# Feed-forward gate and up projections by Strassen's seven products, with the inner activations kept in float32

## The chip, the cores and the metric

The kernel runs on one core of a Trainium2 chip. The metric is the device time of one execution in microseconds (us); less is better. The time before is 1957.03 us, the median of three runs (1954.57 to 1961.09).

Five engines work beside each other and synchronise by semaphores: TensorE (PE: matmuls, and PEld: the loads of their stationary operand), VectorE (DVE), ScalarE (ACT), GpSimd (POOL) and SyncE (SP), which issues the DMAs. Each takes its own instructions strictly in the order in which the program lists them.

## The reference, cut to what matters

Two transformer-like blocks on 512 tokens of width 1024, all in float32. The part that changes is the feed-forward layer, which occurs twice (ffn1 after the first block, ffn2 at the very end):

```python
D_MODEL, SEQ, D_FF = 1024, 512, 2816

def swiglu(h, w_gu, w_down):          # w_gu: 1024 x 5632, w_down: 2816 x 1024
    gu = h @ w_gu
    g, u = jnp.split(gu, 2, axis=-1)
    return (jax.nn.silu(g) * u) @ w_down

f = swiglu(rmsnorm(h, ffn1_pre_g[l]), ffn1_w_gu[l], ffn1_w_down[l])
h = h + 0.5 * rmsnorm(f, ffn1_post_g[l])
```

## The kernel before

Every float32 product is made of three matmuls on a pair of tiles. `split` (line 79) writes a rounded copy `hi` (ScalarE, line 82) and the rest `lo = x - hi` (VectorE, line 83). A product is then hi·hi + hi·lo + lo·hi, summed in PSUM. So a weight tile arrives by DMA in a buffer `raw` (three buffers of 128x1024), is split into `whi` and `wlo`, and feeds TensorE.

In a feed-forward layer (`ffn`, line 728) the normalised input lies as the pair `a_hi`, `a_lo`, transposed, four blocks of 128 tokens by eight blocks of 128 channels. The hidden width is worked off in 11 steps of 256 columns; a step makes 256 columns of the gate g and 256 of u.

- The first step is `lead_T` (line 170): its matmuls (line 187) have 256 columns of tokens, so that it can start on tokens 0 to 255 while the norm of tokens 256 to 511 is still being made. That norm, per block of 128 tokens, is a chain VectorE, POOL, VectorE, ScalarE, VectorE, POOL, VectorE: POOL does one small instruction in it twice (`rp_r`, line 76, a power on 128x1).
- The other ten steps are two calls of `proj_T` each (line 143; matmuls at line 164): two weight tiles of 128x1024, and 2 column halves x 8 channel blocks x 3 = 48 matmuls of 512 columns. The result in PSUM is evacuated by silu on ScalarE (line 741) for g, by a multiplication on VectorE (line 748) for u, and the product is split into `hid_hi`, `hid_lo` at once.
- The down projection is `proj_X` (line 194; matmuls at line 209) through `post_pre` (line 257), in two halves of 512 output columns; the stationary operand is `hid_hi`/`hid_lo`, the moving one the weights.

A scheduler of the Tile framework sets, when the kernel is built, the order in which each engine's instructions stand. It moves instructions of different loop steps past each other, and the tile pools decide which buffer a tile takes over, hence which earlier reader a write must wait for.

Of the kernel before, what the change touches and what calls it, by code (L numbers as in the profile page):

```python
# [7 lines left out]
F32 = mybir.dt.float32  # L8
# [23 lines left out]
def block_kernel(ctx, tc, A, out, upto=99):  # L32
# [134 lines left out]
            for j in range(nj):  # L167
                consume(cc // 128 + j, banks[j][:min(128, w - j * 128), :nt * 128])

    def lead_T(groups, get, slots, splits=((0, 2), (2, 4))):  # L170

        hls = []
        for src, c0, _ in groups:
            hls.append([wload(src, kc, 4, c0, 256, slots.pop(0)) for kc in (0, 4)])
        banks = [[bank() for _ in range(2)] for _ in groups]
        for si, (t0, t1) in enumerate(splits):
            if si:
                flush()
            for g, (_, _, consume) in enumerate(groups):
                for kc in range(2):  # L180
                    hi, lo = hls[g][kc]
                    for j in range(2):
                        for k in range(4):
                            xh, xl = get(kc * 4 + k, t0, t1)
                            wh, wl = hi[:, k, j * 128:j * 128 + 128], lo[:, k, j * 128:j * 128 + 128]
                            for n, (a, b) in enumerate(((wh, xh), (wh, xl), (wl, xh))):
                                PE.matmul(banks[g][j][:, t0 * 128:t1 * 128], a, b, start=(kc + k + n + si == 0),  # L187
                                          stop=(kc == 1 and k == 3 and n == 2), skip_group_check=True)
                                tick((t1 - t0) * 128)
                if t1 == NT:  # L190
                    for j in range(2):
                        consume(j, banks[g][j])

    def proj_X(src, c0, w, get, consume, K=8, nt=NT, tail=1, kp=2, korder=None, between=None, slots=(), ready=None):

# [58 lines left out]
        else:  # L254
            later(delay, lambda: transpose_split(h, 8, pair, t))

    def post_pre(src, K, get, g_post, half_scale, g_pre, fg, last=False, dst=None, korder=None, slots=(), tail=1, delay=DELAY):

        gpost = gain(g_post)
        gpre = None if last else gain(g_pre)  # L260
        x_sb = xb["x"]
        sss = [None] * NT
        pair = None if last else (dst() if dst else new_act())
        mul, eps = (4.0 / D, 4.0 * EPS) if half_scale else (1.0 / D, EPS)

        def evac(hf):
            def f(t, bank):
                fgt = fg[:, t if hf == 0 else NT + t % 2]
                ss = sm.tile([128, 2], F32, name=f"pss{t}", bufs=1) if hf == 0 else sss[t]
                sss[t] = ss  # L270
                ACT.activation(fgt, bank, AF.Square, accum_out=ss[:, hf:hf + 1])
                V.tensor_tensor(fgt, bank, gpost[:, hf * 512:(hf + 1) * 512], op=ALU.mult)  # L272
                if hf == 1:
                    s2 = sm.tile([128, 1], F32, name="s2")
                    V.tensor_tensor(s2, ss[:, 0:1], ss[:, 1:2], op=ALU.add)
                    r = rpow(s2, mul, eps)
                    for q in range(2):
                        xs = x_sb[:, t, q * 512:(q + 1) * 512]
                        V.scalar_tensor_tensor(xs, fg[:, t if q == 0 else NT + t % 2], r, xs, op0=ALU.mult, op1=ALU.add)  # L279
                        if last:  # L280
                            nc.sync.dma_start(out[0].rearrange("(t p) d -> p t d", p=128)[:, t, q * 512:(q + 1) * 512], xs)
                    if not last:
                        prenorm_tile(x_sb[:, t], gpre, pair, t, None, delay)
            return f
        for hf in range(2):
            proj_X(src, hf * 512, 512, get, evac(hf), K=K, korder=korder, tail=max(tail, len(slots)) if hf else 1, slots=slots if hf else ())
        if delay is None:
            flush()
        return pair
# [11 lines left out]
    def first_block():  # L301
# [413 lines left out]
        def of_mb(i):  # L715
            def f():
                if not wmb:
                    wmb[0] = n2.tile([128, 4, 1024], F32R, name="wmb", tag="mb")
                return wmb[0][:, 2 * i], wmb[0][:, 2 * i + 1]
            return f  # L720
        pr = post_pre(A["w_out"], 8, act_get(mg), "norm_post", False, "ffn1_pre_g_2", fg, slots=(two("att0", "att1"), of_mb(0), of_mb(1)))
        st.close()
        return pr
# [4 lines left out]
    def ffn(pair, n, nxt, last=False):  # L728
        st = ExitStack()
        l1 = pool(f"f{n}a", 1, stack=st)  # L730
        l2 = pool(f"f{n}b", 2, stack=st)
        get = act_get(pair)
        w_gu, w_dn = A[f"ffn{n}_w_gu_2"][0], A[f"ffn{n}_w_down_2"][0]
        KF = DFF // 128
        hid = [[l1.tile([128, 2, 512], F32R, name=f"hid_{x}{f}") for x in ("hi", "lo")] for f in range(KF // 2)]
        sg = {}

        def ev_g(f0):
            def f(j, bank):
                s = l2.tile([128, 512], F32, name="sg")  # L740
                ACT.activation(s, bank, AF.Silu)
                sg[f0 + j] = s
            return f

        def ev_u(f0):
            def f(j, bank):
                s = sg.pop(f0 + j)
                V.tensor_tensor(s, s, bank, op=ALU.mult)
                split(hid[f0 // 2][0][:, j], hid[f0 // 2][1][:, j], s)
            return f  # L750
        def hget(k, t0, t1):
            return [x[:, k % 2, t0 * 128:t1 * 128].rearrange("p (t q) -> p t q", q=128) for x in hid[k // 2]]

        def slot(i):
            return lambda: [l1.tile([128, 1024], F32R, name="wsl", tag=f"hid_{x}{i}") for x in ("hi", "lo")]
        lead_T(((w_gu, 0, ev_g(0)), (w_gu, DFF, ev_u(0))), get, [None, None, slot(KF // 2 - 2), slot(KF // 2 - 1)])
# [4 lines left out]
        fg = l1.tile([128, 6, 512], F32, name="fg")  # L761
        pr = post_pre(w_dn, KF, hget, f"ffn{n}_post_g_2", True, nxt, fg, last=last, slots=[slot(i) for i in range(4)])
        st.close()
        return pr

# [3 lines left out]
    def mixer(pair, st):  # L769
# [345 lines left out]
        fg = l1.tile([128, 6, 512], F32, name="fg", tag="u2")  # L1115
        tails = [lambda: [x1.tile([128, 1024], F32R, name=f"wsl{i}") for i in range(2)]]
        g1, g2 = act_get(osT), act_get(oaT, 8)

# [28 lines left out]
    def cross(pair, l1, x1, kT, vm, st):  # L1147
# [9 lines left out]
        for hq in range(2):  # L1157
# [28 lines left out]
            for h in (hq * 2, hq * 2 + 1):  # L1186
                for e in range(2):
# [4 lines left out]
                                      start=(m + a + b == 0), stop=(m + a == 2))  # L1192
                    split(oT[0][:, :, h * 2 + e], oT[1][:, :, h * 2 + e], ob.rearrange("p (t q) -> p t q", t=NT))
        fg = l1.tile([128, 6, 512], F32, name="fg", tag="u2")
        wpt = {}

        def of(tag, i):
# [92 lines left out]
```

## Time and profile before

| | |
|---|---|
| time of three runs | 1957.03 us median, 1954.57 to 1961.09 |
| the profiled execution | 1957.59 us, span 1955.8 us |
| granted TensorE clock, mean | 0.995 |
| TensorE busy | 1903.7 us, 97% of the span |
| VectorE, ScalarE, POOL busy | 1003.9, 708.7 and 38.3 us |
| ffn1: lead step, ten steps, down projection begin at | 580.65, 598.21, 815.84 us |
| ffn2: the ten steps, down projection begin at | 1611.67, 1829.29 us |

The profile is that of one execution. Busy time says how long an engine had an instruction in flight; what limits the time is read from the chain of waits, which is followed back from the last instruction, at each step to what released it. A stretch in which the chain is one long run of matmuls is a stretch in which TensorE sets the pace.

### The profile page before, as it was taken

To read this page: it belongs to the slowest core of one execution; us is meant where nothing else is said; L and a number is where in the kernel's file an instruction comes from. 1 tells how busy PE (TensorE), PEld (TensorE's weight loads), DVE (VectorE), ACT (ScalarE), POOL (GpSimd) and SP (SyncE) were. 2 spreads that over 40 slices of the span, in tenths; PEclk is the share of its full clock that TensorE was granted. 3 is DMA by queue.
4 is the path that set the end of the run, shared out by engine and by line. 5 is a ranking of instruction groups with operands and counts; after the bars stand their busy time and mean duration, and the time that the engine had idled before them with its cause. 6 is when DMAs were issued, how large, how long until landed. Compare 5 with 4: busy or idle time off the path is not lost.

```text
span 1955.8 us, 24155 instructions
## 1 busy us (share of the span) xinstructions
PE 1903.7 (97%) x9676; PEld 1557.1 (80%) x9676; DVE 1003.9 (51%) x1712; ACT 708.7 (36%) x1190; POOL 38.3 (2%) x66
## 2 busy tenths in 40 slices
PE   7999999999999999999999999989999999999998
PEld 6778888788878888888877777667788888888887
DVE  5578833724563333323668666785464553333223
ACT  4345533223343222223545433344353432323221
POOL 0000000100000000000000000000000000000000
PEclk9999999999999999999999999999999999999999
DMA  7411033232332333333231355442262322333332
GB/s 244 130 44 34 24 106 97 88 97 87 105 100 85 97 96 97 96 96 124 83 88 44 87 134 130 125 119 76 83 192 82 99 63 87 97 97 98 97 97 86
DMA packets 153560, 191.10 MB, mean 98 GB/s; under 512 B 9732, under 2 KB 111464, under 8 KB 153320
## 3 DMA queue, kind: packets, MB, share of 16 engines
q1 hardware_dynamic: 153448, 189.56, 32.2%
q8 instruction: 76, 1.25, 0.3%
q14 instruction: 36, 0.29, 0.0%
HBM read 174.85 MB, written 2.10 MB: 90 GB/s over the span
## 4 chain that ended last, share of the span: by engine, by line
PE 81%; DVE 11%; ACT 1%; POOL 1%; issue 1%; DMA 1%; POOLq 0%; DVEq 0%; SPq 0%; ACTq 0%
PE mm L164 41%; PE mm L209 27%; PE mm L187 3%; DVE E L1067 2%; POOL rp_r L76 1%; DVE x_sb L279 1%; DVE l L1070 1%; PE ob L538 1%; DVE h L251 1%; DVE wlo L83 1%; PE s L561 1%; PE ob L924 1%; PE s L1165 1%; DVE fg L272 1%; PE mm L579 1%
## 5 line engine op out<-in xcount | busy, mean ns | idle before, releaser
L83 DVE TENSOR_TENSOR wlo<-raw,whi 128x1024 fp32r<-128x1024 f32 (+1 forms) x274 | 333.6, 1217 | 675.6 <-ACT whi L82 670.1
L82 ACT ACTIVATE whi<-raw 128x1024 fp32r<-128x1024 f32 (+1 forms) x274 | 289.0, 1055 | 692.7 <-PE mm L164 296.7
L164 PE MATMUL mm<-a_hi,wlo 128*128 128x512 f32 x1120 | 439.1, 392 | 1.9 <-DVE wlo L83 1.9
L164 PE MATMUL mm<-a_hi,whi 128*128 128x512 f32 x1120 | 440.3, 393 | 0.0
L164 PE MATMUL mm<-a_lo,whi 128*128 128x512 f32 x1120 | 439.3, 392 | 0.0
L164 PEld LDWEIGHTS mm<-a_hi,wlo 128*128 128x128 f32 x1120 | 210.8, 188 | 46.0 <-DVE wlo L83 2.4
L164 PEld LDWEIGHTS mm<-a_hi,whi 128*128 128x128 f32 x1120 | 210.7, 188 | 44.5 <-issue 2.0
L164 PEld LDWEIGHTS mm<-a_lo,whi 128*128 128x128 f32 x1120 | 210.9, 188 | 43.5 <-issue 1.7
L209 PE MATMUL mm<-whi,a_hi 128*128 128x512 f32 (+1 forms) x384 | 150.6, 393 | 2.2 <-ACT a_hi L82 2.2
L209 PE MATMUL mm<-whi,a_lo 128*128 128x512 f32 (+1 forms) x384 | 151.1, 393 | 0.0
L209 PE MATMUL mm<-wlo,a_hi 128*128 128x512 f32 (+1 forms) x384 | 149.5, 391 | 0.0
L209 PE MATMUL mm<-whi,hid_hi 128*128 128x512 f32 x288 | 112.0, 389 | 0.0
L209 PE MATMUL mm<-whi,hid_lo 128*128 128x512 f32 x288 | 112.0, 389 | 0.0
L209 PE MATMUL mm<-wlo,hid_hi 128*128 128x512 f32 x288 | 112.0, 389 | 0.0
L209 PEld LDWEIGHTS mm<-whi,a_hi 128*128 128x128 f32 x384 | 72.7, 189 | 19.0 <-ACT a_hi L82 2.8
L209 PEld LDWEIGHTS mm<-whi,a_lo 128*128 128x128 f32 x384 | 72.8, 189 | 15.2 <-issue 2.3
L209 PEld LDWEIGHTS mm<-wlo,a_hi 128*128 128x128 f32 x384 | 72.5, 189 | 14.3 <-issue 1.6
L76 POOL TENSOR_TENSOR rp_r<-rp_a,half 128x1 f32<-128x1 f32 (+1 forms) x58 | 36.8, 635 | 1891.2 <-DVE rp_a L74 1571.7
L209 PEld LDWEIGHTS mm<-whi,hid_lo 128*128 128x128 f32 x288 | 54.1, 188 | 11.3
L209 PEld LDWEIGHTS mm<-whi,hid_hi 128*128 128x128 f32 x288 | 54.1, 188 | 11.2
L209 PEld LDWEIGHTS mm<-wlo,hid_hi 128*128 128x128 f32 x288 | 54.1, 188 | 11.2
L1067 DVE TENSOR_TENSOR_SCAN E<-l,own 128x128 f32<-128x128 f32 (+2 forms) x64 | 49.6, 811 | 8.3 <-ACT l L1058 8.3
(446 smaller groups left out, 2846.6 us busy)
## 6 DMA issues: line engine op xcount, KB each, us to landing
raw<-in_w_in_dram SPq DMA_DIRECT2D x96, 512.0 KB, 3.7
raw<-in_ffn_w_gu_dram SPq DMA_DIRECT2D x88, 512.0 KB, 3.5
raw<-in_ffn_w_down_dram SPq DMA_DIRECT2D x44, 512.0 KB, 3.7
raw<-in_w_out_dram SPq DMA_DIRECT2D x24, 512.0 KB, 3.8
raw<-in_xa_wkv_dram SPq DMA_DIRECT2D x16, 512.0 KB, 4.2
raw<-in_w_ret_o_dram SPq DMA_DIRECT2D x8, 512.0 KB, 3.4
K<-kh SPq DMA_DIRECT2D x32, 128.0 KB, 2.4
K<-kl SPq DMA_DIRECT2D x32, 128.0 KB, 2.3
```

The costliest lines, as they stand in the source:

```text
L76: POOL.tensor_tensor(r[:, :n], a[:, :n], half[:, :n], op=ALU.pow)
L82: ACT.activation(hi, src, AF.Copy)
L83: V.tensor_tensor(lo, src, hi.bitcast(F32), op=ALU.subtract)
L164: PE.matmul(o, a, b, start=(kc + k == 0 and n == 0 and si == 0), stop=(kc + k == K - 1 and n == 2), skip_group_check=True)
L187: PE.matmul(banks[g][j][:, t0 * 128:t1 * 128], a, b, start=(kc + k + n + si == 0), stop=(kc == 1 and k == 3 and n == 2), skip_group_check= ...
L209: PE.matmul(banks[t][:, :w], a, b, start=(kk == 0 and n == 0), stop=(kk == K - 1 and n == 2))
L251: V.scalar_tensor_tensor(h, src, r, g, op0=ALU.mult, op1=ALU.mult)
L272: V.tensor_tensor(fgt, bank, gpost[:, hf * 512:(hf + 1) * 512], op=ALU.mult)
L279: V.scalar_tensor_tensor(xs, fg[:, t if q == 0 else NT + t % 2], r, xs, op0=ALU.mult, op1=ALU.add)
L538: m = PE.matmul(ob[64 * e:64 * e + 64, a], vv[:, j, br, g * 64:(g + 1) * 64], pT[:, e, j], start=False, stop=(br == 1 and j == nk - 1), sk ...
L561: PE.matmul(sbs[e], qS[:, h, qsl], kk[:, br, g, :W], start=(n == 0 and (e == 0 or nk > 2)), stop=(n == 1), skip_group_check=True)
L1067: V.tensor_tensor_scan(E[:, rev], l[:, off + W - 1:(off - 1) if off else None:-1], own1[:, 511:(511 - W) if W < 512 else None:-1], 1.0, op ...
```

## The change

The ten steps behind the lead step no longer call `proj_T`. Each half step (256 columns of g, or of u) is a call of `seven_T`, which takes the product of the weight tile, cut in 2 channel halves by 2 column halves (w11, w12, w21, w22), with the activations, cut in 2 token halves by 2 channel halves, as seven block products after Strassen and Winograd. A block product has 4 channel blocks x 3 = 12 matmuls of 256 columns.

- `seven_of`, once per layer, makes four sums of activation quadrants (operands 5, 7, 6 and 3) and splits them: two additions on POOL, two on VectorE, four more and four `lo` on VectorE, four `hi` on ScalarE, each of 128x1024. They stand between the two halves of the lead step's tokens.
- In `seven_T`, four subtractions of weight blocks (128x512) on POOL make the weights 5, 6, 7 and 4. Weight 1 (128x512), the pair (5, 6), the pair (7, 4) and the pair (2, 3) (128x1024 each) are split. The products run in the order 1, 5, 6, 7, 2, 3, 4 in the four quarters a, b, c, d of two PSUM banks; partial sums u and q and the four output blocks are taken out in between, by one ScalarE copy and VectorE additions of 128x256 (lines 260 to 273).
- g and u are multiplied in SBUF, half of it on POOL (line 870), and stored as one float32 tile `hid` per step. The down projection splits each `hid` tile when it needs it, once in each of its two output halves (`getter`).

```diff
-    def lead_T(groups, get, slots, splits=((0, 2), (2, 4))):
+    def lead_T(groups, get, slots, splits=((0, 2), (2, 4)), ready=None):
...
             if si:
                 flush()
+                if ready:
+                    ready()
...
+    def seven_of(pair, tmp, dst):
+        a = {}
+        for n, (th, kh) in enumerate(((1, 0), (1, 1), (0, 0), (0, 1))):
+            a[th, kh] = tmp(n)
+            (V if th else POOL).tensor_tensor(a[th, kh], quadrant(pair[0], th, kh).bitcast(F32), quadrant(pair[1], th, kh).bitcast(F32), op=ALU.add)
+        ops = {1: tuple(quadrant(x, 0, 0) for x in pair), 2: tuple(quadrant(x, 0, 1) for x in pair), 4: tuple(quadrant(x, 1, 1) for x in pair)}
+
+        def made(n, out, x, y, op):
+            V.tensor_tensor(out, x, y, op=op)
+            hi, lo = dst(n)
+            split(hi, lo, out)
+            ops[n] = (hi, lo)
+            return out
+        s1 = made(5, a[1, 1], a[1, 0], a[1, 1], ALU.add)
+        made(7, a[1, 0], a[0, 0], a[1, 0], ALU.subtract)
+        s2 = made(6, a[0, 0], s1, a[0, 0], ALU.subtract)
+        made(3, a[0, 1], a[0, 1], s2, ALU.subtract)
...
+    def seven_T(src, c0, ops, wop, snap, c11, outs, done):
+        raw0, r0 = wraw(src, 0, 4, c0, 256)
+        raw1, r1 = wraw(src, 4, 4, c0, 256)
+        w11, w12, w21, w22 = r0[:, :, 0:128], r0[:, :, 128:256], r1[:, :, 0:128], r1[:, :, 128:256]
...
+        split(W[1][0], W[1][1], w11)
+        POOL.tensor_tensor(t12[:, 0], w12, w11, op=ALU.subtract)
+        POOL.tensor_tensor(t12[:, 1], w22, t12[:, 0], op=ALU.subtract)
+        two(t12.rearrange("p a k c -> p (a k c)"), (5, 6))
+        POOL.tensor_tensor(t34[:, 0], w22, w12, op=ALU.subtract)
+        POOL.tensor_tensor(t34[:, 1], w21, t12[:, 1], op=ALU.subtract)
+        two(t34.rearrange("p a k c -> p (a k c)"), (7, 4))
+        hi, lo = wop["two"]()
+        split(hi, lo, raw1)
...
+        def product(n, r, first=False):
+            for k in range(4):
+                xh, xl = ops[n](k)
+                wh, wl = W[n][0][:, k], W[n][1][:, k]
+                for i, (a, b) in enumerate(((wh, xh), (wh, xl), (wl, xh))):
+                    PE.matmul(reg[r], a, b, start=(first and k + i == 0), stop=(k == 3 and i == 2), skip_group_check=True)
+                    tick(256)
+        u, q = snap("u"), snap("q")
+        product(1, "a", True)
+        ACT.copy(u, reg["a"])
+        product(5, "c", True)
+        product(6, "b")
+        V.tensor_tensor(u, u, reg["b"], op=ALU.add)
+        V.tensor_tensor(q, u, reg["c"], op=ALU.add)
+        product(7, "d")
+        V.tensor_tensor(outs(1, 1), q, reg["d"], op=ALU.add)
+        product(2, "a")
+        c11(reg["a"])
+        product(3, "c")
+        V.tensor_tensor(outs(0, 1), u, reg["c"], op=ALU.add)
+        done(0)
+        product(4, "d")
+        V.tensor_tensor(outs(1, 0), u, reg["d"], op=ALU.add)
+        done(1)
...
-        for f0 in range(2, KF, 2):
-            proj_T(w_gu, f0 * 128, 256, get, ev_g(f0))
-            proj_T(w_gu, DFF + f0 * 128, 256, get, ev_u(f0))
...
+            def done_u(step):
+                x, y = (h[:, 1], g[:, 1]) if step == 0 else (half(h, 1, 0), half(g, 1, 0))
+                (V if step else POOL).tensor_tensor(x, x, y, op=ALU.mult)
...
+                    have[k // 2] = [l1.tile([128, 2, 512], F32R, name="xd", tag=f"s{n}{x}") for x in "hl"]
+                    split(*have[k // 2], hid[k // 2])
```

The rest of the diff hands buffers about (the weights of product 1 lie in the two `gain` buffers, the four pairs of the other weights in `whi`/`wlo` and `whi2`/`wlo2`) and writes the tile `fg` as a list.

VectorE in the middle of ffn1's ten steps, before: `sg` is the gate in SBUF, `mm` a PSUM bank, `hid` the split product; a row with `wlo` is the `lo` of one weight tile.

```order
L83 TENSOR_TENSOR wlo_5678<-raw_5675,whi_5677 128x1024
L748 TENSOR_TENSOR sg_5601<-sg_5601,mm_5605 128x512
L83 TENSOR_TENSOR hid_lo4_4866<-sg_5601,hid_hi4_4865 128x512
L748 TENSOR_TENSOR sg_5603<-sg_5603,mm_5606 128x512
L83 TENSOR_TENSOR wlo_5708<-raw_5705,whi_5707 128x1024
L83 TENSOR_TENSOR hid_lo4_4866<-sg_5603,hid_hi4_4865 128x512
L83 TENSOR_TENSOR wlo_5744<-raw_5741,whi_5743 128x1024
```

The same place after, one half step of g (its tiles are `raw_5885`, `raw_5887`, `u_5912`, `q_5913`, banks `mm_5910` and `mm_5911`). `whi_5906`, `wlo_5907` are its weights (2, 3); `gain_6136` is weight 1 of the half step after the next; `whi2_6024`, `wlo2_6025` are the weights (7, 4) of the next.

```order
L83 TENSOR_TENSOR wlo_5907<-raw_5887,whi_5906 128x1024
L83 TENSOR_TENSOR gain_6136<-raw_6130,gain_6136 128x512
L263 TENSOR_TENSOR u_5912<-u_5912,mm_5910 128x256
L264 TENSOR_TENSOR q_5913<-u_5912,mm_5911 128x256
L83 TENSOR_TENSOR wlo2_6025<-h_6012,whi2_6024 128x1024
L266 TENSOR_TENSOR G_5884<-q_5913,mm_5911 128x256
L270 TENSOR_TENSOR G_5884<-u_5912,mm_5911 128x256
L83 TENSOR_TENSOR wlo_6029<-raw_6009,whi_6028 128x1024
L273 TENSOR_TENSOR G_5884<-u_5912,mm_5911 128x256
L83 TENSOR_TENSOR wlo_6142<-h_6134,whi_6141 128x1024
```

Where a half step had two `lo` and one evacuation per PSUM bank, it now has three and a half `lo` and five small evacuations. The sums u and q stand behind the `lo` of weight 1 of the half step after the next, and the sum behind product 7 (line 266) stands behind the `lo` of the next half step's weights (7, 4).

POOL at the entry of ffn1, before: all that it does there is the power `rp_r` of the norm, twice for each block of 128 tokens; the fifth row is the last of that norm.

```order
L76 TENSOR_TENSOR rp_r_4744<-rp_a_4742,half_89 128x1
L76 TENSOR_TENSOR rp_r_4785<-rp_a_4783,half_89 128x1
L76 TENSOR_TENSOR rp_r_4794<-rp_a_4792,half_89 128x1
L76 TENSOR_TENSOR rp_r_4835<-rp_a_4833,half_89 128x1
L76 TENSOR_TENSOR rp_r_4844<-rp_a_4842,half_89 128x1
L76 TENSOR_TENSOR rp_r_7098<-rp_a_7096,half_89 128x1
```

The same place after; `st` are the quadrant sums of `seven_of`, `h` and `wt` the weight differences of the first half steps.

```order
L76 TENSOR_TENSOR rp_r_4794<-rp_a_4792,half_89 128x1
L76 TENSOR_TENSOR rp_r_4835<-rp_a_4833,half_89 128x1
L206 TENSOR_TENSOR st_5032<-a_hi_4488,a_lo_4489 128x1024
L206 TENSOR_TENSOR st_5034<-a_hi_4488,a_lo_4489 128x1024
L76 TENSOR_TENSOR rp_r_4844<-rp_a_4842,half_89 128x1
L238 TENSOR_TENSOR h_5154<-raw_5150 128x512
L239 TENSOR_TENSOR h_5154<-raw_5152,h_5154 128x512
L241 TENSOR_TENSOR h_5155<-raw_5152,raw_5150 128x512
L242 TENSOR_TENSOR h_5155<-raw_5152,h_5154 128x512
L238 TENSOR_TENSOR wt_5276<-raw_5272 128x512
```

The two quadrant sums of tokens 0 to 255 now stand between the last two powers of the norm; behind the last power POOL's queue is weight differences, four for each half step, to the end of the ten steps.

## Rows read from the trace of the kernel before

**Rows 1.** The page's first part: busy us, share of the span, instructions, by engine.
```profile
PE 1903.7 (97%) x9676; PEld 1557.1 (80%) x9676; DVE 1003.9 (51%) x1712; ACT 708.7 (36%) x1190; POOL 38.3 (2%) x66
```
**Rows 2.** The chain of waits, its long pieces: start us, us, what.
```profile
580.65 17.56 PE mm L187 x140
598.21 217.63 PE mm L164 x960
815.84 103.37 PE mm L209 x456
...
951.35 13.33 PE mm L187 x112
...
1431.04 12.02 PE mm L164 x103
...
1611.67 217.63 PE mm L164 x960
```
**Rows 3.** Busy time in three stretches: lead step, ten steps, ffn2's down projection.
```profile
core 0: us, PE busy (x) PEld busy (x) DVE busy (x) ACT busy (x) POOL busy (x), PEclk, DMA share, GB/s
580.65:598.21 17.56, 17.56 (x142) 17.56 (x141) 4.67 (x7) 5.69 (x7) 0.00 (x0) 0.95 0.42 138
598.21:815.84 217.63, 217.63 (x961) 180.19 (x961) 75.19 (x80) 63.98 (x80) 0.00 (x0) 1.00 0.31 95
...
1829.29:1948.98 119.69, 119.68 (x529) 98.79 (x527) 36.50 (x42) 27.15 (x36) 1.65 (x3) 1.00 0.29 93
```
**Rows 4.** VectorE's groups, 598.21 to 815.84: busy us, mean ns; idle before, releaser.
```profile
L83 DVE TENSOR_TENSOR wlo<-raw,whi 128x1024 fp32r<-128x1024 f32 x39 | 47.8, 1226 | 122.1 <-ACT whi L82 122.1
L83 DVE TENSOR_TENSOR hid_lo<-sg,hid_hi 128x512 fp32r<-128x512 f32 x21 | 14.5, 690 | 8.4 <-ACT hid_hi L82 8.4
```
**Rows 5.** ScalarE's groups in the same stretch.
```profile
L82 ACT ACTIVATE whi<-raw 128x1024 fp32r<-128x1024 f32 x40 | 42.5, 1061 | 107.0 <-PE mm L164 72.3 <-issue 34.7
L82 ACT ACTIVATE hid_hi<-sg 128x512 fp32r<-128x512 f32 x20 | 12.5, 623 | 27.4 <-DVE sg L748 27.4
```
**Rows 6.** A group of 128x256 from PSUM on VectorE, whole span.
```profile
L83 DVE TENSOR_TENSOR kT<-mm,kT 128x256 fp32r<-128x256 f32 x8 | 3.3, 418 | 0.0
```
**Rows 7.** A group of 128x256 from PSUM on ScalarE, whole span.
```profile
L82 ACT ACTIVATE kT<-mm 128x256 fp32r<-128x256 f32 x8 | 3.0, 376 | 4.1 <-PE mm L164 4.1
```
**Rows 8.** POOL's instructions in order of time: start us, us, what, idle before.
```profile
20.67 1.46 POOL L76 TENSOR_TENSOR rp_r<-rp_a,half 128x1 f32<-128x1 f32 x1 [2.13 <-DVE rp_a L74]
25.34 0.32 POOL L376 COPY vv<-kvt 128x128 f32<-128x128 f32 x1 [3.21 <-ACT kvt L373]
...
573.31 0.55 POOL L76 TENSOR_TENSOR rp_r<-rp_a,half 128x1 f32<-128x1 f32 x1 [2.32 <-DVE rp_a L74]
```
**Rows 9.** VectorE's instructions in order of time, around the first two of those.
```profile
20.51 1.22 DVE L83 TENSOR_TENSOR wsl<-raw,wsl 128x1024 fp32r<-128x1024 f32 x1
...
25.42 0.26 DVE L352 TENSOR_TENSOR rp<-kvt,cb_t 128x16 f32<-128x16 f32 x1
...
27.72 0.17 DVE L352 TENSOR_TENSOR rp<-kvt,cb_t 128x16 f32<-128x16 f32 x1
```
**Rows 10.** DMA issues: KB each, median us from issue to landing.
```profile
raw<-in_ffn_w_gu_dram SPq DMA_DIRECT2D x88, 512.0 KB, 3.5
```
**Rows 11.** The chain of waits at the entry of ffn1, last token block.
```profile
573.90 1.42 DVE x_sb L279 x2
...
576.83 0.56 POOL rp_r L76
...
577.41 1.29 DVE h L251
...
578.75 1.05 PE s L236 x4
```

More of the change, by code (lines that the diff above doesn't have):

```diff
@@ L734, in ffn @@
         KF = DFF // 128
[L735 to L750, printed above, removed]
@@ L761, in ffn, with ev_g @@
-        fg = l1.tile([128, 6, 512], F32, name="fg")
-        pr = post_pre(w_dn, KF, hget, f"ffn{n}_post_g_2", True, nxt, fg, last=last, slots=[slot(i) for i in range(4)])
+        NP = KF // 2
+        hid = [l1.tile([128, 2, 512], F32, name=f"hid{f}") for f in range(NP)]
+        SEVEN = (5, 6, 7, 3)
+        seven = {n: [l1.tile([128, 2, 4, 128], F32R, name=f"s{n}{x}") for x in "hl"] for n in SEVEN}
+        turns = {"two": 0, "tmp": 0}
+        G = {}
+        def ev_g(j, bank):
+            if j == 0:
+                G[0] = l2.tile([128, 2, 512], F32, name="G")
+            ACT.activation(G[0][:, j], bank, AF.Silu)
@@ new lines, in ev_u, with slot, two @@
+        def ev_u(j, bank):
+            V.tensor_tensor(hid[0][:, j], G[0][:, j], bank, op=ALU.mult)
+        def slot(*i):
+            return lambda: [l1.tile([128, 1024], F32R, name="wsl", tag=f"hid{f}") for f in i]
+        def two():
+            n = turns["two"] = turns["two"] + 1
+            if n % 4 < 2:
+                return wp.tile([128, 1024], F32R, name="whi"), wp.tile([128, 1024], F32R, name="wlo")
+            return l2.tile([128, 1024], F32R, name="whi2"), l2.tile([128, 1024], F32R, name="wlo2")
@@ new lines, in one, with tmp, ready @@
+        def one():
+            t = gp.tile([128, D], F32R, name="gain")
+            return t[:, 0:512], t[:, 512:1024]
+        def tmp():
+            n = turns["tmp"] = turns["tmp"] + 1
+            return l1.tile([128, 1024], F32, name="wt") if n % 3 == 0 else hp.tile([128, D], F32, name="h")
+        wop = {"two": two, "one": one, "tmp": tmp}
+        ops = {}
+        def ready():
+            ops.update(seven_of(pair, lambda n: l1.tile([128, 2, 4, 128], F32, name="st", tag=f"hid{NP - 5 - n}"), lambda n: seven[n]))
@@ L763, in ffn @@
+        f2 = [l2.tile([128, 2, 512], F32, name="G") for _ in range(2)] + [l1.tile([128, 2, 512], F32, name="wt")]
+        fg = [f2[i // 2][:, i % 2] for i in range(6)]
+        pr = post_pre(w_dn, KF, None, f"ffn{n}_post_g_2", True, nxt, fg, last=last, slots=[slot(0, 1), slot(2, 3), slot(4, 5)], tail=4,
+                      gets=[getter(), getter()])
         st.close()
@@ L1115, in mixer @@
         fg = l1.tile([128, 6, 512], F32, name="fg", tag="u2")
+        fg = [fg[:, i] for i in range(6)]
         tails = [lambda: [x1.tile([128, 1024], F32R, name=f"wsl{i}") for i in range(2)]]
@@ L1194, in cross @@
         fg = l1.tile([128, 6, 512], F32, name="fg", tag="u2")
+        fg = [fg[:, i] for i in range(6)]
         wpt = {}
```

52 lines of the change are left out of this document (43 added, 9 removed).

## The prediction

> **What bounds the kernel now.** I read the page's first part, then the chain of waits, then the busy time by stretch, then the groups of VectorE and ScalarE inside the stretch that changes. TensorE is busy 97% of the span, POOL 2% [rows 1]. The chain shows where that matters: in each feed-forward layer it runs as one piece of 960 matmuls over the ten steps, 217.63 us, and then through the down projection [rows 2]. So nothing else is on the path there, and a half step (48 matmuls of 512 columns) costs 217.63 / 20 = 10.88 us. In that stretch VectorE works 75.19 us of 217.63, ScalarE 63.98, POOL nothing, at a granted clock of 1.00, the upper level of 2.4 GHz [rows 3]; VectorE's idle time ends with ScalarE's `whi` and ScalarE's with a matmul [rows 4, 5], so both only follow. Fewer TensorE columns there would be worth their whole time as long as the others keep up.
>
> **TensorE's side.** A half step has 7 x 12 = 84 matmuls of 256 columns in place of 48 of 512: 21504 columns for 24576, seven eighths. The duration is not seven eighths, since a short matmul costs more than half of a long one: 13.33 us / 112 = 0.119 us in one run of 256 columns, 12.02 / 103 = 0.117 in another, against 217.63 / 960 = 0.2267 for 512 [rows 2]. Why shows in the weight loads: busy 180.19 of 217.63 us at 512 columns, but 17.56 of 17.56 in the lead step, which has 256 [rows 3]. By half of the long one, 0.1134, a half step would be 9.52 us; by the row it is 84 x 0.119 = 10.00 us, which I take. The Trainium skill (Perfetto Trace Analysis, Identifying the Most-Contended Engine) says to judge TensorE's headroom by the share of LDWEIGHTS and not of matmuls; by it the new stretch has no headroom left at 256 columns, and the trace agrees with its 100%. Saving: 40 half steps x (10.88 - 10.00) = 35 us. That is the whole possible gain.
>
> **VectorE's chain in a half step.** A product's first matmul waits for the evacuation that read the other quarter of its bank: product 2 for u, 7 for q, 3 and 4 for the two outputs. In VectorE's order u stands behind the `lo` of weights (2, 3), 1.226 us, and of a later weight 1, 0.690 [rows 4]. With the other engines free: when the half step before ends, ScalarE needs 1.061 for the `hi` of (2, 3) (its buffer comes free only then, in every second half step), then a copy of 0.376 [rows 7] and 0.623 [rows 5]; VectorE ends the first `lo` at about 2.5, the second at 3.2 and u (0.418 [rows 6], after product 6) at 3.7. TensorE has 31 matmuls until it needs u, 3.7 us. Later waits are covered in the same way by five or seven matmuls of other products in between. So this chain costs some 0.2 us a half step, by a hair. ScalarE's work is 0.62 + 3 x 1.06, the copy and the silu, some 4.9 us of 10, and hides.
>
> **POOL and the port.** New on POOL are 4.5 operations of 128x512 a half step, four subtractions and every second time a multiplication. No row has such a form. From below it is VectorE's 0.690 for the same shape [rows 4]; from above POOL's copy, 0.32 us for 128x128 [rows 8], times four for the elements and two for the second input, 2.56. I take 4 x 0.32 = 1.28: the row's own rate, its fixed part paying for the second input. That is 5.8 us a half step, within 10. The Trainium skill (GPSIMD Engine Reference, 3.1) gives 4497 ns for such an addition of 2048 elements, so 1.12 us as an estimate; the forecast would then come out 6 us lower, and no row here shows it.
>
> But POOL and VectorE don't run beside each other where both read SBUF. At 20.67 a `rp_r`, 0.55 alone, takes 1.46 us and ends 0.40 after a VectorE subtraction of two SBUF tiles that ran from 20.51 to 21.73; at 25.42 a VectorE operation that takes 0.17 alone takes 0.26 and ends with POOL's copy at 25.66 [rows 8, 9]. Each waits for the other. A half step's VectorE operations on two SBUF tiles are 0.69 + 3 x 1.226 and half of 0.42, 4.6 us; with POOL's 5.8 the shared path is taken 10.3 of TensorE's 10.0 us. The five evacuations from PSUM (2.1 us) may run beside POOL. With the path full, POOL's operations must stand in front of VectorE's `lo` often: POOL holds about half of the time, a half step has three `lo` with an evacuation behind them, and the cover of 0.6 us is spent. I charge one POOL operation to the chain, 1.28. Bounds: 0 (they fall into VectorE's idle time) to three, 3.84. Half step: 10.00 + 0.2 + 1.28 = 11.5 us against 10.88. Both charges: 40 x 1.48 = 59 us.
>
> **DMA.** The same bytes in the same tiles. The buffers turn in a longer loop: the `lo` of (2, 3) frees a `raw` buffer, a transfer of 3.5 us [rows 10] fills it, POOL does two subtractions, that frees another `raw`, whose transfer carries the weight 1 that stands ahead of u in the next half step but one. Added up, over two half steps: 1.3 + 1.2 + 3.6 + 2 x 1.28 + 3.6 + 0.7 + 0.8 + 0.4 and 6.3 for the rest of the products, with 0.4 of gaps, 20.9 us. That is 10.4 a half step, below 11.5, so it adds nothing by itself; every wait for the port on it does, which is a second reason for the charge.
>
> **Entry of a layer.** POOL's two quadrant sums of 128x1024, 2 x 2.56 = 5.1 us, stand between the last two `rp_r`. From the one's end (573.9) to the other's start (576.83) there are 2.96 us, and behind it are h and the transposes for which TensorE's queue waits [rows 11]. So 2.2 us late at least; since the two x_sb operations at 573.90 read two SBUF tiles and wait for the first sum, I take 4. Bound: 5.1 and the VectorE work pushed behind, 7. Then VectorE makes the four operands: ten operations of 1.226, four more such for the first weights and three of 0.69, about 19 us, while TensorE has 96 + 41 matmuls, 16.3 us: 3 us late, up to 6 with POOL in the way. Together 7 a layer, 14 us for two.
>
> **Down projection.** It takes 22 more splits of 128x1024 a layer, 27 us of VectorE and 23 of ScalarE, beside 36.5 and 27.2 that it has in 119.69 us [rows 3]; four buffers run ahead. They hide. The last half step has no later product to fill its waits: 1 us a layer, 2. What `proj_T` did with `hid`, 0.69 and 0.62 a tile, is gone and was hidden.
>
> **Sum.** 1957.6 (the profiled execution, 0.03% above the median) - 35 + 59 + 14 + 2 = 1997.6; against the median I say **1997 us**, 2% slower. The whole turns on the charge per half step: break-even is (35 - 16) / 40 = 0.48 us.
>
> **The rivals.**
> *POOL fits into the gaps.* VectorE waits for nothing but itself, a half step is 10.2, the entry costs 2.2 + 1.2: -35 + 8 + 7 + 2 = -18, 1939 us. For it: VectorE's own work is 6.9 of 10 us, POOL's operations come in a bunch when a `raw` lands, and every second half step has its weights (2, 3) early. Against it: both halves of the exclusion [rows 8, 9], and a sum of 10.3. It wins if the charge stays under 0.48.
> *POOL is the bound.* Above about 1.55 us an operation, 4.5 of them with VectorE's 4.6 exceed 11.5 us a half step. At 1.92, midway to the upper bound: 13.2, +93, the entry 20 and 2: 2072 us. For it: nothing in the trace but the upper bound; the copy's 0.32 contains a wait for VectorE, which speaks against.
> *The short matmuls are slower than 0.119.* In the lead step 140 pieces took 17.56 us, 0.125 each [rows 2]; with all seven products so, a half step is 0.5 longer, hence 2018 us. Most of the saving is then gone: the change does not do what its count of columns says. Against it: that piece contains transposes and the last weight's arrival.
>
> **How the numbers follow.** The forecast 0.47 (its own range 1965 to 2035: charge 0.9 to 2.2 and the entry's bounds), POOL in the gaps 0.28, POOL as the bound 0.15, slower matmuls 0.10. A measurement can tell 0.3%, 6 us. Slower: the forecast less its low edge (0.41), 0.15 and 0.09: 0.65. Same: 0.06, 0.01 and 0.04 from the gaps case: 0.11. Faster: the rest of that case, 0.24. Range: down to 1930, where the gaps case also loses the entry's cost, up to 2060, where POOL as the bound begins; about 0.15 is left out.
>
> **What would show it.** In the changed kernel's chain of waits the two ten-step stretches should no longer be one piece of matmuls: VectorE (`lo` and the sums of lines 263 to 273) and POOL should hold a part of them, the stretch from lead step to down projection should be near 230 us, not 217.6, and TensorE's idle time should be ended by u, q and the outputs. VectorE's `lo` of 128x1024 should show a mean well above 1.23, or POOL's 128x512 well above 1.28, where they collide. At the entry, h of the last token block should come about 4 us later behind POOL's sums. I am wrong if POOL's 128x512 lies under 1.0 with VectorE's rows unchanged, if the chain stays on TensorE through the stretch at 200 to 205 us (the gaps case), or if TensorE's matmuls alone make the loss.

## The result, and the profile after

The changed kernel takes 2005.42 us, the median of four runs (2001.54 to 2008.69), against 1957.8 us for the kernel before on the same chip: 1.0242 times as long, 95% interval 1.0217 to 1.0268. The forecast was 1997 us.

The profiled execution has a span of 2006.9 us, 51.1 more than the 1955.8 of before. The first part of its page, to be read against [rows 1]:

```profile
PE 1903.9 (95%) x11116; PEld 1613.0 (80%) x11116; DVE 1268.8 (63%) x2012; ACT 812.5 (40%) x1338; POOL 317.7 (16%) x250
```

TensorE's busy time hardly changed, so the eighth of the ten steps' columns that went is not gained as time. The chain of waits no longer holds the ten steps as one piece of matmuls, as it did in [rows 2]; this is a cut of 23 us from their middle (start, duration, what):

```profile
692.67 0.34 DVE u L263
...
701.39 2.32 DVE wlo L83
...
703.73 3.67 DMA raw<-in_ffn_w_gu_dram
...
707.53 1.30 POOL wt L239
708.83 1.26 POOL h L241
...
710.11 3.58 DMA raw<-in_ffn_w_gu_dram
...
714.38 1.28 DVE gain L83
715.67 0.34 DVE u L263
```

The chain is the turn of the raw buffers that the prediction listed: `lo`, transfer, two subtractions, transfer, weight 1, u. From one u to the next but one there are 23.0 us, 11.5 a half step. What makes it long can be read from the rows of POOL and VectorE side by side (two timelines; the three POOL rows come first):

```profile
689.83 2.30 POOL L238 TENSOR_TENSOR h<-raw 128x512 f32<-128x512 f32 x1 [2.43 <-DMA raw<-in_ffn_w_gu_dram]
701.13 1.49 POOL L870 TENSOR_TENSOR hid<-hid,G 128x512 f32<-128x512 f32 x1
707.53 1.30 POOL L239 TENSOR_TENSOR wt<-raw,wt 128x512 f32<-128x512 f32 x1 [4.91 <-DMA raw<-in_ffn_w_gu_dram]
```
```profile
689.75 1.23 DVE L83 TENSOR_TENSOR wlo<-h,whi 128x1024 fp32r<-128x1024 f32 x1 [0.61 <-ACT whi L82]
690.89 1.78 DVE L83 TENSOR_TENSOR gain<-raw,gain 128x512 fp32r<-128x512 f32 x1
701.39 2.31 DVE L83 TENSOR_TENSOR wlo<-raw,whi 128x1024 fp32r<-128x1024 f32 x1
703.63 0.68 DVE L83 TENSOR_TENSOR gain<-raw,gain 128x512 fp32r<-128x512 f32 x1
```

POOL alone takes 1.30 us (707.53; 1.28 was assumed). At 689.83 it takes 2.30, since VectorE's `lo` runs until 690.98, and then VectorE's 0.68 takes 1.78, since POOL holds on until about 692.1. At 701.39 a `lo` of 1.23 takes 2.31: POOL ends at 702.62, and 1.08 us later the `lo` ends. (That POOL row is the multiplication of line 870, not a subtraction; it collides in the same way.) Over the stretch of 602.1 to 840.77 us, against [rows 4] and with what TensorE waited for (group: busy, mean ns | idle; and waits: total, times, longest):

```profile
L83 DVE TENSOR_TENSOR wlo<-raw,whi 128x1024 fp32r<-128x1024 f32 x22 | 40.3, 1830 | 7.3 <-ACT whi L82 7.1
L83 DVE TENSOR_TENSOR gain<-raw,gain 128x512 fp32r<-128x512 f32 x19 | 22.6, 1188 | 3.8 <-ACT gain L82 3.8
```
```profile
PE mm L256 <- DVE u L263: 14.2, 18, 1.6
```

For the `lo` of weights (2, 3), which stands ahead of u, 1.23 us became 1.83 on average; those of the two pairs of differences are at 1.39 and 1.41. The `lo` of weight 1 went from 0.69 to 1.19, and nearly all that TensorE waits is for u. The Trainium skill (SBUF — State Buffer, Who interferes with whom) says that a VectorE instruction with two SBUF inputs and a GpSimd instruction that reads SBUF exclude each other, and that the loser blocks for the whole of the other; the rows agree.

For one number per kernel I use the pitch of u: 20 of them in a layer, from the first start to the last, divided by 19 (duration min/median/max, first and last start):

```profile
L263 DVE TENSOR_TENSOR u<-u,mm x20: 406/408/421, 611.9 to 830.1; 128x256 f32<-128x256 f32 x20
L263 DVE TENSOR_TENSOR u<-u,mm x20: 405/407/422, 1651.0 to 1873.7; 128x256 f32<-128x256 f32 x20
```

That is 11.48 and 11.72 us a half step in the two layers, 11.60 on average, for 10.88 before: 40 x 0.72 = 29 us of the 51. (The first of the 19 intervals in each layer, 12.2 and 14.7 us, still belongs to the entry; the other eighteen average 11.44 and 11.56.) The other 22 are at the entries. In the chain at the entry of ffn1, against [rows 11], and with POOL's row beside it:

```profile
571.86 0.55 POOL rp_r L76
...
572.43 5.63 DVE x_sb L361 x2
...
579.59 0.86 POOL rp_r L76
...
587.89 1.77 POOL h L239
...
596.63 2.24 DVE s5l L83
598.87 2.23 DVE st L210
601.10 2.24 DVE s7l L83
```
```profile
572.37 5.15 POOL L206 TENSOR_TENSOR st<-a_hi,a_lo 128x1024 f32<-128x1024 f32 x2
```

The two x_sb take 5.63 us in place of 1.42, because POOL's two sums of quarters run beside them; h begins 8.07 us after this rp_r's end, before it was 3.54. Then the operands are made one behind the other, several at 2.24 for 1.23, beside the first weights' subtractions. The lead step ends 5.35 us later than before, counted from the end of rp_r (the first one shown), and the first u comes 39.5 us after it. In ffn2 the two x_sb run ahead of POOL's sums and take 1.41 us, but rp_r waits behind the sums: h begins 3.8 us later than before, and the first u comes 39.0 us after rp_r.

TensorE's clock falls at the entries too. In ffn1 the granted clock is 0.78 from 582 to 592 us, after 9.6 us of which TensorE had been busy for 3.6; from 607 to 611.9 us, after TensorE had stood idle for 2.3 us, it is 0.66, with matmuls 0.213 us apart in place of 0.12 until 610.1 us: these run at 1.2 GHz, the lower of the two levels. In ffn2 it is 0.66 from 1651 to 1661 us, after waits of 1.4 and 0.9 us. Over the rest of the ten steps it is 1.00, so the pitch of u is not the clock's doing beyond its first interval. At these places the chain runs through VectorE, POOL and transfers; what the clock adds to the 22 us no run shows apart.

### The profile page after: what moved, and what is told of

Its sections match the earlier page's. It is cut to its first block, busy times and chain, and to the rows that moved or that the text cites. A ratio compares the mean times of both kernels' runs of the same rounds, so it can differ in the third digit from the quotient of the medians.

```text
span 2006.9 us, 27815 instructions
## 1 busy us (share of the span) xinstructions
PE 1903.9 (95%) x11116; PEld 1613.0 (80%) x11116; DVE 1268.8 (63%) x2012; ACT 812.5 (40%) x1338; POOL 317.7 (16%) x250
## 3 DMA queue, kind: packets, MB, share of 16 engines
q8 instruction: 87, 1.43, 0.3%
## 4 chain that ended last, share of the span: by engine, by line
PE 63%; DVE 17%; DMA 6%; POOL 4%; issue 3%; ACT 3%; SPq 0%; DVEq 0%; POOLq 0%; ACTq 0%
PE mm L291 26%; PE mm L164 18%; PE mm L256 8%; DMA raw<-in_ffn_w_gu_dram 5%; DVE wlo L83 4%; DVE E L1197 2%; DVE gain L83 2%; ACT whi L82 2%; DVE x_sb L361 1%; POOL rp_r L76 1%; DVE l L1200 1%; PE ob L620 1%; PE mm L189 1%; POOL h L241 1%; DVE h L333 1%
## 5 line engine op out<-in xcount | busy, mean ns | idle before, releaser
L164 PE MATMUL mm<-a_hi,wlo 128*128 128x512 f32 x480 | 191.0, 399 | 1.9 <-DVE wlo L83 1.9
L164 PE MATMUL mm<-a_hi,whi 128*128 128x512 f32 x480 | 192.0, 400 | 0.0
L164 PE MATMUL mm<-a_lo,whi 128*128 128x512 f32 x480 | 190.7, 397 | 0.0
L291 PE MATMUL mm<-whi,xd 128*128 128x512 f32 x608 | 188.7, 390 | 1.6 <-DVE hid L273 0.9
L291 PEld LDWEIGHTS mm<-whi,xd 128*128 128x128 f32 x608 | 113.9, 188 | 26.4 <-DVE hid L273 1.8
L256 PE MATMUL mm<-a_hi,whi 128*128 128x256 f32 x320 | 99.1, 310 | 30.4 <-DVE u L263 30.4
L291 PE MATMUL mm<-wlo,xd 128*128 128x512 f32 x304 | 118.4, 389 | 0.0
L164 PEld LDWEIGHTS mm<-a_hi,wlo 128*128 128x128 f32 x480 | 91.0, 190 | 21.0 <-DVE wlo L83 2.4
L164 PEld LDWEIGHTS mm<-a_lo,whi 128*128 128x128 f32 x480 | 91.1, 190 | 19.0 <-issue 1.7
L256 PE MATMUL mm<-a_hi,wlo 128*128 128x256 f32 x320 | 90.9, 284 | 0.0
```

The source lines that it names most:

```text
L164: PE.matmul(o, a, b, start=(kc + k == 0 and n == 0 and si == 0), stop=(kc + k == K - 1 and n == 2), skip_group_check=True)
L256: PE.matmul(reg[r], a, b, start=(first and k + i == 0), stop=(k == 3 and i == 2), skip_group_check=True)
L291: PE.matmul(banks[t][:, :w], a, b, start=(kk == 0 and n == 0), stop=(kk == K - 1 and n == 2))
```

## The experiments

The theory at the outset: POOL's operations cost about 1.4 us a half step, by the port and by their place in the loop of raw buffers. The rivals: the bank scheme's waits, slow short matmuls, the loop alone. Ratios are against the kernel before, run on the same chip.

**The subtractions left out.** All four go:

```diff
-POOL.tensor_tensor(t12[:, 0], w12, w11, op=ALU.subtract)
...
-two(t12.rearrange("p a k c -> p (a k c)"), (5, 6))
+two(raw0, (5, 6))
-two(t34.rearrange("p a k c -> p (a k c)"), (7, 4))
+two(raw1, (7, 4))
```

> The four POOL subtractions of each half step are left out: the operand pairs (5, 6) and (7, 4) are split straight from the two weight tiles, so the gate and up sums are not those of the reference. Everything else stays: 84 matmuls, three splits, the sums of the quarters. My theory (POOL's operations, by the port that they share with VectorE and by their place in the loop of the raw buffers, cost about 1.4 us a half step): a half step falls from 11.6 to 10.2 us, 40 x 1.4 = 56 us less than the changed kernel, about 1950 us, and VectorE's splits of 128x1024 come back to 1.23 us. Rival 'the waits of the bank scheme': the products wait for u, q and the outputs whatever POOL does, a half step stays at 11 us or more, 1980 us or more. Rival 'short matmuls are slow': TensorE is busy without a gap at 10.5 us or more, 1962 us or more.

1951.66 us, ratio 0.9987 (0.9978 to 0.9996). The u of its first layer (the second has the same 201.6 us from first to last) and its busy time over some 19 half steps of that layer:

```profile
L258 DVE TENSOR_TENSOR u<-u,mm x20: 414/421/422, 605.4 to 807.0; 128x256 f32<-128x256 f32 x20
```
```profile
601.06:804.72 203.66, 203.66 (x1622) 196.61 (x1620) 134.66 (x192) 88.20 (x125) 11.66 (x9) 1.00 0.33 102
```

The time is that of the theory: by the two ratios 50 us go with POOL's subtractions. The half step is not: it is 10.61 us and not 10.2, and TensorE is listed as busy throughout, as the rival of slow matmuls had it (10.5 or more). So this order of products is worth 40 x 0.27 = 11 us at best, not 35. VectorE's `lo` of 128x1024 come back to 1.33 us on average, not quite to 1.23; POOL's multiplication is still there. Most of the eleven go at the entries, where the first u still comes 4.1 us late in ffn1 and 4.7 in ffn2.

**The subtractions made short.**

```diff
-POOL.tensor_tensor(t12[:, 0], w12, w11, op=ALU.subtract)
+POOL.tensor_tensor(t12[:, 0, :, :n12], w12[:, :, :n12], w11[:, :, :n12], op=ALU.subtract)
```

> The four POOL subtractions stay in their places with all their waits, but from the fourth tile on each works on 16 of the 128 columns of a block (128x64 in place of 128x512), and the splits behind them read what lies there; the sums are not those of the reference. The order of all instructions and the turns of the buffers stay. My theory (the time for which POOL holds the port and the chain is what costs): about 10.2 us a half step, 1950 us, as without the subtractions. Rival 'the order': the in-order wait of VectorE for a split that stands behind POOL's and the longer turn of the raw buffers cost in themselves, however short POOL's work is: 11 us or more a half step, 1980 us or more.

1964.28 us, ratio 1.0049 (1.0032 to 1.0066); u from 611.0 to 813.7 and from 1627.4 to 1829.9, 10.67 and 10.66 us a half step. The order, the dependencies and the turn of the buffers are those of the changed kernel, and cost 0.05 us. So the time for which POOL is at work is what costs; the rival 'order' falls. The first u comes 37.6 us after rp_r, 4.8 later than without subtractions, where the first six subtractions of a layer are still whole; twice 4.8 is most of the 12.6 us between the two medians.

**A fourth raw buffer.**

```diff
-raw0, r0 = wraw(src, 0, 4, c0, 256)
+raw0, r0 = wraw(src, 0, 4, c0, 256, wop["raw"]())
+def more():
+    n = turns["raw"] = turns.get("raw", -1) + 1
+    return l1.tile([128, 1024], F32, name=f"raw{n % 4}") if n % 4 >= 3 else None
```

> The feed-forward steps get a fourth raw buffer (every fourth weight tile lies in a tile of the layer's own pool); POOL's subtractions stay whole. It computes the reference. Theory 'port': POOL's 5.8 us and VectorE's 4.6 us on pairs of SBUF tiles exclude each other, 10.4 us of a half step whatever the buffers do; the half step stays above 11 us, 1980 to 2005 us. Rival 'loop': two transfers of 3.6 us and two POOL operations in the turn of three buffers set the pace; with a fourth buffer the transfers start earlier, a half step falls to 10.2 to 10.5 us and the whole to 1950 to 1962 us.

2016.92 us, ratio 1.0316 (1.0295 to 1.0338): a little slower still, and above the 1980 to 2005 us forecast, with 11.66 and 11.91 us a half step. Its chain has no transfer left in two half steps, only the collision in front of u:

```profile
700.39 2.31 DVE wlo L83
702.70 1.67 DVE gain L83
704.37 0.34 DVE u L263
...
704.75 15.25 PE mm L256 x120
```

The rival 'loop' falls: without the two transfers on the chain the same `lo` and weight 1, stretched from 1.23 and 0.69 to 2.31 and 1.67, hold u up. TensorE waits for u 9 times for 18.6 us, in place of 18 times for 14.2. By the pitch some 7 us of the difference lie in the half steps, and the first u comes 41.2 us after rp_r, 1.7 later; why was not pursued.

**Short matmuls alone, in the kernel before.**

```diff
-proj_T(w_gu, f0 * 128, 256, get, ev_g(f0))
+proj_T(w_gu, f0 * 128, 256, get, ev_g(f0), splits=((0, 2), (2, 4)))
```

> The kernel before, with the matmuls of the gate and up projections cut in two column halves: 96 matmuls of 256 columns in place of 48 of 512 in each of the 40 half steps, nothing else changed. By the pitch of the changed kernel's matmuls (0.1195 us) a half step takes 11.47 in place of 10.88 us: 24 us more than before, 1981 us. If a short matmul costs exactly half of a long one: 1957 us. If it costs 0.125 as in the lead step: 12.0 a half step, 2002 us.

1977.51 us, ratio 1.0119 (1.0097 to 1.014), 23 us more, as forecast from the pitch. Its ten steps are dense:

```profile
597.07:827.47 230.40, 230.40 (x1922) 230.40 (x1921) 72.84 (x80) 64.85 (x80) 0.00 (x0) 1.00 0.28 90
```

230.40 / 1920 = 0.1200 us a matmul, with the weight loads busy 100%. So 84 of them are 10.08 us, and the other 0.53 of the 10.61 above must be gaps, which the listed durations of the matmuls hide. They can be seen in the starts in the kernel without subtractions, which are 0.12 apart except in a few places, of which this is one (start, duration; x2 stands for two starts):

```profile
690.01 0.40 PE L251 MATMUL mm<-a_hi,gain 128*128 128x256 f32 x2
690.25 0.28 PE L251 MATMUL mm<-a_lo,gain 128*128 128x256 f32 x1
690.51 0.39 PE L251 MATMUL mm<-a_hi,whi 128*128 128x256 f32 x1
690.74 0.28 PE L251 MATMUL mm<-a_lo,whi 128*128 128x256 f32 x1
```

0.25 us are lost where product 2 (the rows with `whi`) waits for u behind five matmuls of cover (0.6 us): its first matmul starts 0.14 late, the next another 0.11. VectorE is free there: u starts at 690.04, right behind product 6, and ends at 690.46. The same happens at product 4 (0.18), and in every second half step at product 6 (0.18), which has twelve matmuls of cover but waits for ScalarE's copy, late behind a silu. Together that is 0.52 a half step, the 0.53 looked for.

**The entry sums on VectorE, behind the last h.**

```diff
-(V if th else POOL).tensor_tensor(a[th, kh], quadrant(pair[0], th, kh).bitcast(F32), quadrant(pair[1], th, kh).bitcast(F32), op=ALU.add)
+s = V.tensor_tensor(a[th, kh], quadrant(pair[0], th, kh).bitcast(F32), quadrant(pair[1], th, kh).bitcast(F32), op=ALU.add)
+after(s, xb["h"])
```

> The changed kernel with one thing different at the entry of a layer: all four sums of the operand quarters run on VectorE, behind the last h, none on POOL. In the changed kernel's trace h comes 4.5 us later than before, behind POOL's two sums, and the lead step ends 5.35 us later. Theory: what delays the entry is POOL's sums in front of rp_r and the port that they take from x_sb; h comes back to where it was, two sums of 1.23 us are added to VectorE's queue for the operands, and each layer gains 3 to 4.5 us: 6 to 9 us less than the changed kernel, 1996 to 1999 us. Rival: VectorE's queue of operands is what TensorE waits for at the entry, and it becomes longer by 2.5 us; no gain, 2003 us or more.

1999.0 us, ratio 1.0218 (1.0197 to 1.0239), which the intervals don't separate from the changed kernel's. The trace shows the gain: the two x_sb take 2.44 us, and the first u comes 36.5 us after rp_r, 3.0 earlier.

```profile
572.10 2.44 DVE x_sb L362 x2
```

**Only the float32 activations.**

```diff
-seven_T(w_gu, f * 256, ops, wop, snap, lambda p: ACT.activation(half(g, 0, 0), p, AF.Silu), lambda th, j: half(g, th, j), done_g)
+proj_T(w_gu, f * 256, 256, get, lambda j, bank: ACT.activation(g[:, j], bank, AF.Silu))
...
```

> Only the second half of the change: the inner activations lie in float32 and are split in the down projection (22 more splits of 128x1024 a layer), but gate and up are computed as before by 48 matmuls of 512 columns a half step, and no operand sums are made. Theory: the splits hide beside TensorE, the time is that of the kernel before within 0.3%, 1951 to 1961 us. Rival: the two VectorE and ScalarE queues at the start of the down projection or the four turning buffers make TensorE wait; 3 us or more a layer, above 1961 us.

1957.83 us, ratio 1.0006 (0.9993 to 1.0019). The splits in the down projection hide, to within the interval.

**The subtractions on VectorE, all and half of them.** The first kernel moves all four, the second those of lines 238 and 239:

```diff
-POOL.tensor_tensor(t12[:, 0], w12, w11, op=ALU.subtract)
+V.tensor_tensor(t12[:, 0], w12, w11, op=ALU.subtract)
...
```

> The changed kernel with the four weight subtractions on VectorE in place of POOL; it computes the reference. VectorE's own work in a half step grows from 7.1 us (144 us in 216.6 us of the run without the subtractions, 20 half steps) by 4 x 0.69 to 9.8 us, against TensorE's 10.6. Theory 'port': without POOL nothing collides, VectorE just fits, a half step 10.6 to 10.9 us: 1952 to 1965 us. Rival 'VectorE is full': the sums of the quarters stand behind subtractions for which TensorE then waits, 11.2 us or more a half step: 1976 us or more.

> As before it, but only the first two subtractions (those that make the pair 5, 6) go to VectorE; the other two stay on POOL. POOL then works 3.2 us a half step, VectorE 8.5. Theory 'port': fewer collisions, but those that stay meet a fuller VectorE; a half step of 10.8 to 11.3 us, 1960 to 1985 us, between the changed kernel and the one with all four on VectorE. Rival: the collisions that cost are those of the last two subtractions, which run beside the splits that stand ahead of u; no gain, 2000 us or more.

All four: 1958.57 us, ratio 1.0003 (0.9994 to 1.0013), u from 606.7 to 810.6, 10.73 and 10.70 us a half step. Two of four: 2003.37 us, ratio 1.0233 (1.0211 to 1.0254), 11.89 and 11.76. VectorE has room for all the work, but half of POOL's does as much harm as all of it: the forecast for the half was wrong, and its rival right in the time. In the half kernel the third subtraction, on POOL, meets the second, moved to VectorE:

```profile
714.15 1.28 POOL L241 TENSOR_TENSOR wt<-raw 128x512 f32<-128x512 f32 x1 [4.86 <-DVE gain L83]
```
```profile
714.24 1.74 DVE L239 TENSOR_TENSOR h<-raw,h 128x512 f32<-128x512 f32 x1
```

The subtraction at 714.24 (0.69 alone) stands ahead of q, for which TensorE now waits 3.5 us in this layer, besides 9.2 for u (14.2 in the changed kernel). So the rival's reason, the splits ahead of u, is only part of it: other waits have come in their place.

**Subtractions and entry sums on VectorE.** Both edits above.

> The changed kernel with both earlier edits: the four weight subtractions and all four entry sums on VectorE, the sums behind the last h. It computes the reference. Theory: the two add up; from 1958.6 us with the subtractions alone, 3 to 4.5 us less in each layer, 1950 to 1953 us, which is less than the kernel before. Rival: at the entry VectorE has the subtractions of the first half steps and the sums in one queue, and TensorE waits for the operands instead: 1957 us or more.

1950.97 us, ratio 0.9978 (0.9966 to 0.9991). The second edit gains on top of the first, 0.25% with separate intervals, which is 2.4 us a layer and not the 3 to 4.5 forecast. The two x_sb are back at 1.42 us and the first u comes 27.8 us after rp_r, for 34.4 with the subtractions alone; but in ffn1 the half steps are then longer, 10.97 us for 10.73, and of the 6.5 us the last u keeps 1.9 (3.3 in ffn2).

**Longer cover, with POOL as it was.** Other quarters share a bank, and product 2 comes last:

```diff
-reg = {"a": bx[:, 0:256], "b": bx[:, 256:512], "c": by[:, 0:256], "d": by[:, 256:512]}
+reg = {"a": bx[:, 0:256], "d": bx[:, 256:512], "c": by[:, 0:256], "b": by[:, 256:512]}
 product(7, "d")
...
-product(2, "a")
-c11(reg["a"])
 product(3, "c")
...
 product(4, "d")
+product(2, "a")
+c11(reg["a"])
```

> The changed kernel, POOL and all, with another use of the two PSUM banks and another order of the products: quarters a and d lie in one bank, c and b in the other, and the order is 1, 5, 6, 7, 3, 4, 2, so that no product starts before 12 matmuls have passed since the one whose evacuation it waits for. Theory 'cover': the run without subtractions shows two gaps of about 0.25 us a half step where five matmuls of cover are too few (10.61 in place of 84 x 0.12 = 10.08 us), and the waits for u that the collisions make last 0.8 us on average; 12 matmuls, 1.44 us, cover both: a half step of 10.2 to 10.7 us, 1950 to 1968 us. Rival 'throughput': POOL and VectorE together are full whatever TensorE waits for; a half step stays at 11.2 us or more, 1988 us or more.

1970.08 us, ratio 1.007 (1.0045 to 1.0095), 10.71 and 10.81 us a half step. By the ratios 34 us of the loss go although POOL does all that it did and the collisions stay. The stretched `lo` are partly others: those of a difference are at 1.58 us (1.39 in the changed kernel), those of weights (2, 3) at 1.43 (1.83), and weight 1 at 1.08 (1.19):

```profile
L83 DVE TENSOR_TENSOR wlo<-h,whi 128x1024 fp32r<-128x1024 f32 x25 | 39.5, 1580 | 2.3 <-ACT whi L82 2.3
L83 DVE TENSOR_TENSOR gain<-raw,gain 128x512 fp32r<-128x512 f32 x19 | 20.5, 1078 | 0.8 <-ACT gain L82 0.8
```

So the rival 'throughput' falls: the two engines are not full, and a collision costs by its place ahead of an evacuation with too little cover. In ffn1 TensorE no longer waits for u at all. It came out 2 us above the range given for it; the entry is unchanged (first u 39.4 us after rp_r). How much of the 34 us is the collisions, and how much the gaps that were there without them, the next run shows.

**All three edits.** The new order of products, with the subtractions and the entry sums on VectorE.

> The same order of products, with the weight subtractions and the entry sums on VectorE. It computes the reference. Theory 'cover': the gaps of 0.53 us a half step go, TensorE runs at 0.12 us a matmul, 10.1 to 10.3 us a half step: 16 to 24 us less than with the subtractions alone on VectorE, and the entry's 3 to 4.5 us a layer: 1928 to 1937 us, over 1% less than the kernel before. Rival 'VectorE is full': 9.8 us of its own work against 10.1, its queue falls behind, 10.6 us or more a half step: 1947 us or more.

1935.87 us, ratio 0.9884 (0.9856 to 0.9911): 1.2% faster than the kernel before, clear of the interval. A half step is 10.40 and 10.29 us in the two layers, a little above the 10.1 to 10.3 forecast. In the middle of ffn1 TensorE is listed as busy throughout four half steps, 10.25 us each:

```profile
719.05:760.03 40.98, 40.97 (x336) 40.51 (x336) 34.63 (x57) 18.60 (x26) 3.23 (x2) 1.00 0.33 104
```

The 0.17 us beyond 84 x 0.12 = 10.08 are gaps at the start of product 3, some 0.2 us in most of these half steps, read from the starts of its matmuls. Product 3 waits for q, since a weight subtraction now stands between u and q on VectorE and waits for its transfer; here it is at 719.05, where 0.33 us are lost:

```profile
717.97 0.69 DVE L240 TENSOR_TENSOR wt<-raw,wt 128x512 f32<-128x512 f32 x1 [0.21 <-DMA raw<-in_ffn_w_gu_dram]
718.58 0.41 DVE L265 TENSOR_TENSOR q<-u,mm 128x256 f32<-128x256 f32 x1
```
```profile
718.70 0.28 PE L257 MATMUL mm<-a_lo,gain 128*128 128x256 f32 x1
719.05 0.39 PE L257 MATMUL mm<-s3h,whi 128*128 128x256 f32 x1
```

On average of the two layers the new order takes 0.84 us from a half step with POOL's subtractions (11.60 to 10.76) and 0.37 to 0.47 without them (to 10.35, from 10.72 with the subtractions alone on VectorE and from 10.82 with the entry sums there too). So of the 34 us above some 15 to 19 are gaps that were there without POOL's subtractions, and only the rest is what the collisions cost. That cost falls from 0.8 or 0.9 us a half step in the old order to 0.41 in the new (10.76 - 10.35): longer cover hides about half of it, not all.

## Why the prediction was right, and what in it was not

- *Direction, size and main cause: right.* POOL's subtractions collide with VectorE's `lo` ahead of u. Without them the kernel is at 1951.66 us. The half step was forecast at 11.5 us and is 11.60. The forecast is 8 us short, and that is mostly the entry. The stretch from lead step to down projection in ffn1, said to be near 230 us, takes 238.7, with part of the entry's loss in it.
- *TensorE's half step, 10.00 + 0.2: too low.* It is 10.61. The matmul's 0.119 was right (0.1200), but the cover of the waits, called enough "by a hair", is too short, and each wait with five matmuls of cover costs about 0.2 us. The prediction counted VectorE's queue from the start of the half step; what binds without POOL's subtractions is the way from the end of product 6 through u to product 2. So "the whole possible gain" was 11 us, not 35, and the rival in which POOL fits into the gaps (1939) couldn't have come true in this order even with POOL gone. The rival of short matmuls had the right size, half a microsecond a half step, with the wrong reason.
- *The charge for the port, 1.28: too high by a quarter.* 11.60 - 10.61 = 0.99. This and the term before it erred in opposite directions; that their sum came so near, 11.48 for 11.60, is luck.
- *The loop of raw buffers "adds nothing by itself": right*, as the fourth buffer and the short subtractions show. The stretched loop is what the chain shows, but when the loop is broken the cost comes back in front of u without it.
- *POOL's 1.28 for 128x512: right*, 1.30 where nothing collides; the 1.92 of the rival in which POOL is the bound is out.
- *Entry, 7 us a layer: too low.* h comes 4.5 us later in ffn1, 3.8 in ffn2 (4 forecast). Where the first u would come 28.7 us after rp_r (the lead step's 24.34 of before, and the 4.3 that u stands behind it without subtractions), it comes at 39.5: 10.8 us a layer. Making the operands costs some 6.3 us, not the 3 taken but near the 6 given "with POOL in the way", since the operands and the first weights' subtractions collide. What the fallen clock has in it is not separated.
- *Down projection hidden: right*, ratio 1.0006. The exit's 1 us a layer was not measured by itself.

The sum from measured terms: 40 x 0.72 = 29, and 2 x 10.8 = 22, together 51; the spans differ by 51.1.

What stays open: why the fourth buffer made it slower still, and what TensorE's clock costs at the entries.

## What to carry to other kernels

Before counting a saving in matmul columns, count for every product the matmuls that stand between an evacuation and the product that waits for it: here five did not cover an evacuation even when VectorE was free, and twelve mostly did, also a delayed one. Longer cover took 34 us from the changed kernel, and about 18 from the one without POOL's subtractions and sums; the saved columns could give 40 x (10.88 - 10.08) = 32 at most. Work moved to POOL wasn't free here, where VectorE subtracts pairs of SBUF tiles: what mattered most was which instruction the collision stands ahead of, and the fuller VectorE was better here than the shared load. A loop that fills the chain of waits needs an experiment that breaks it before it is called the cause. And a stretch in which TensorE is listed as busy throughout can still hold gaps: here they showed only in the starts of the matmuls.

## What the runs showed of the hardware that was not expected

- A collision of POOL and VectorE costs both: POOL's 1.30 becomes 2.30 and VectorE's 1.23 becomes 2.31, depending on which was first. Two VectorE operations of 0.7 us each took 5.63 together beside two POOL sums of 128x1024.
- Half of POOL's subtractions were as dear as all of them (11.83 and 11.60 us a half step on average); with all of them on VectorE it is 10.72.
- An evacuation of 0.42 us isn't covered by five matmuls of 0.12: the product that waits for it loses 0.25 us, 0.14 before its first matmul and 0.11 behind it.
